# Gated-DeltaNet heads and adaLN modulation in a two-layer trunk: the 16x16 solve as its own stage, and the modulation product gathered over K

## The chip, the core and the metric

One core of a Trainium2 chip runs the whole kernel. The metric is the device time of one execution in microseconds (us). The engines are PE (TensorE, the matrix engine), DVE (VectorE), ACT (ScalarE), POOL (GpSimd) and SP (SyncE, which here only issues transfers). Each takes its own instructions strictly in order and waits for the others through semaphores.

## What is computed

A trunk of two layers, for one prompt of 1024 tokens and eight samples of 8 tokens each (1088 columns in all), with a model width of 1024. Layer 0 mixes tokens with a gated delta rule (GDN, eight heads), layer 1 with a gated linear recurrence (HGRN2, eight heads); each is followed by a convolutional feed-forward block (ConvFFN, 2816 wide). Six modulation vectors for each layer come from one product with the conditioning vectors. Cut to what matters here:

```
cs = silu(c)                                        # 9 conditioning rows (prompt + 8 samples)
for layer in range(2):
    mod = cs @ ada_w[layer] + ada_b[layer]          # 1024 x 6144: sh1, sc1, g1, sh2, sc2, g2
    h = rmsnorm(x) * (1 + sc1) + sh1
    out = gdn(h) or hgrn(h)
    x = x + (1 + g1) * rmsnorm(out)
    h = rmsnorm(x) * (1 + sc2) + sh2
    x = x + (1 + g2) * rmsnorm(conv_ffn(h))

# gated delta rule, per head and chunk of 64 tokens
A = strict_lower(kb @ k.T) * decay
sol = triangular_solve(A + I, [v * beta, kb * exp(G)])
u = uv - w @ S;  o = qg @ S + attn @ u;  S = S * gl + kd.T @ u
```

## The kernel before

**Order.** The program is written in stages, and a list scheduler sets the order on each engine from that written order and the dependences; afterwards an engine never overtakes. A GDN head is a generator, `gdn_head`, with seven stages separated by `yield`: (1) project k, convolve it; (2) decay matrices, k times k, transposes of k, and the solve; (3) project q, multiply it with k and with its decay; (4) project v and the gate g; (5) the merge; (6) the recurrence over eight 128-token tiles; (7) the samples and the output. The main loop interleaves two heads: `stage(h, 2 if h else 3)` brings head h through q and v, then come stage 1 of head h+1, stage 5 of head h, stage 2 of head h+1, and stages 6 and 7 of head h. So the solve of head h+1 is written ahead of the recurrence of head h, and the dense projection matmuls of h+1's q fill PE between the small ones of the recurrence.

**The solve.** The inverse of each 128x128 triangular block is built up from 16x16 blocks. Stage 2 writes the masked k times k to DRAM and reads the 72 diagonal blocks back as one block per partition (Zp, Ep; Ep by a POOL transfer). L794 multiplies them (`fs<-fs,Ep`; fs holds Zp, Lp and the result). L799 and L801 are 15 pairs of a small multiply and a reduce, each needing the one before; L802 copies the result; two transfers on POOL's queue write it to DRAM (`td`, L804) and read it back in the merge's layout (`mg`, L805); four ACT operations mask it (L815, L816). The merge, stage 5, begins with 32x32 matmuls `pV` (L882), whose operand those ACT operations finish, and a DVE product with EM (L875, L883).

**Modulation.** `ada_half` takes 512 of the 1024 rows of ada_w by 256 columns: four matmuls (four K blocks in the four 32-row column groups of PE), a copy by ACT, and later `ada_flush`, in which matmuls with a selector (`sel9`, L158) add the four groups up and DVE adds bias or the earlier half (L161). A 256-column piece has two halves. `ada_step` places four halves in each GDN head, with a flush for each; the ConvFFN of layer 0 takes 16 and the HGRN heads 32, there with one flush for two halves. The first two vectors of layer 0 are made in the prologue.

**Dense matmuls.** Projections and feed-forward go through `dense`: weights and activations are split into a high and a low part, three matmuls for each (L113 to L115), 384, 384 and 320 columns wide.

In time the span is: prologue to about 125 us, eight GDN heads of some 95 us to 906, output projection and norms to 1060, first ConvFFN to 1760, HGRN heads 1890 to 2430, second ConvFFN from 2580 to about 3300.

Of the kernel before, what the change touches and what calls it, by code (L numbers as in the profile page):

```python
# [14 lines left out]
ALU = mybir.AluOpType  # L15
# [27 lines left out]
def trunk_kernel(ctx: ExitStack, tc: tile.TileContext, a: dict, o: dict):  # L43
# [107 lines left out]
    def ada_flush(pt=None):  # L151

        if not ada_late:
            return
        l, c, add, sb = ada_late.pop(0)
        p2 = (pt or ps("mx", name="adap2"))[:, 256:274]
        for j in range(2):
            mm(p2[:, 9 * j:9 * j + 9], sb[:, 128 * j:128 * j + 128], sel9, start=True, stop=True)  # L158
        m = mods[l][:, 2 * c:2 * c + 2, :]
        base = m if add else adab[:, l, 2 * c:2 * c + 2].unsqueeze(2).to_broadcast([128, 2, 9])  # L160
        nc.vector.tensor_tensor(m, p2.rearrange("p (j r) -> p j r", r=9), base, op=ALU.add)  # L161


    def mod(l, i):
# [297 lines left out]
    def ffn(l, hgs, step, nxt, hname, extra, post=None):  # L462
# [3 lines left out]

        def ada_next(extra):
            if extra:
                ada_half(*extra.pop(0), "D10", "mx", True)

        def gate(f, xtag="xp", ctag=None):

# [60 lines left out]
        for c, fs in enumerate(CHUNKS[:-1]):  # L533
            if c == 0:
                gates_up(fs[:3])
                ada_next(extra)
            for f in fs[3 if c == 0 else 0:]:
                gate_up(f)
                ada_next(extra)
            for m in range(8):  # L540
                w = load_w(a["w_dn"][l, c, m], 512, "wd") if len(fs) == 4 else load_w(a["w_d3"][l, 0, m], 384, "wd")
                if c == 0:
                    acc[m] = big(f"A{m}", [128, NT], name=f"facc{m}")
                if c == 0 and m % 2:
# [152 lines left out]
        nc.vector.scalar_tensor_tensor(dst, xp, 1.0, dst, op0=ALU.add, op1=ALU.mult)  # L697
        return xp

    rest = [(0, c, hf) for c in range(8, 24) for hf in range(2)]  # L700

    def ada_step():
        ada_half(*rest.pop(0), "D10", "mm")

    def gdn_head(h):
        par = h % 2
# [84 lines left out]
            out=Zp, in_=zd[par].rearrange("t x -> (t x)").rearrange("(b y) -> b y", y=2064)[:, :2048].rearrange(  # L791
                "b (j i) -> b j i", i=128)[:, :, 0:16])
        nc.gpsimd.dma_start(out=Ep, in_=ed[par])
        nc.vector.tensor_tensor(Lp, Zp.rearrange("p j i -> p i j"), Ep.unsqueeze(2).to_broadcast([72, 16, 16]), op=ALU.mult)  # L794
        nc.gpsimd.memset(Tp, 0.0)
        nc.gpsimd.memset(fs[:72, 512 + 16:1024:33], 1.0)
        for i in range(1, 16):
            pri = fs[:72, 0:i * i].rearrange("p (c j) -> p c j", j=i)
            nc.vector.tensor_tensor(pri, Tp[:, 0:i, 0:i].rearrange("p j c -> p c j"),  # L799
                                    Lp[:, i:i + 1, 0:i].to_broadcast([72, i, i]), op=ALU.mult)  # L800
            nc.vector.tensor_reduce(Tp[:, i, 0:i], pri, axis=mybir.AxisListType.X, op=ALU.add)  # L801
        nc.vector.tensor_copy(Xp, Tp.rearrange("p i c -> p c i"))  # L802
        mg = big("D7", name="mg")
        nc.gpsimd.dma_start(out=td[par], in_=fs[:72, 512:1024])  # L804
        nc.gpsimd.dma_start(out=mg[:, 0:288].rearrange("p (t x) -> p t x", x=32),  # L805
                            in_=td[par].rearrange("(t k) (r x) -> (k r) t x", k=8, x=32))

        cp = mg[:, 0:288].rearrange("p (t i c) -> p t i c", i=2, c=16)
        XTc = mg[:, 288:800].rearrange("p (t i e c) -> p t i e c", i=2, e=2, c=16)
        Xs = mg[:64, 800:832]  # L810
        x32 = mg[:, 288:800].rearrange("p (t i c) -> p t i c", i=2, c=32)
        Xc, Tc = x32[:, :, 0, :], x32[:, :, 1, :]
        EM, V = [mg[:, i:i + 256].rearrange("p (t c) -> p t c", c=32) for i in (0, 832)]
        for e in range(2):
            nc.scalar.activation(XTc[:, :, :, e, :], cp[:, 0:8], AF.Copy, scale=m16e[:, e:e + 1])  # L815
            nc.scalar.activation(Xs[:, 16 * e:16 * e + 16], cp[:64, 8, 0, :], AF.Copy, scale=m16e[:64, e:e + 1])  # L816
        yield

        q = A(0, "q")
# [22 lines left out]
        nc.sync.dma_start(out=eg, in_=gd[1, h:h + 1, :].to_broadcast([128, NTOK]))  # L842
        nc.vector.tensor_tensor(q, q, eg, op=ALU.mult)
        qg = q

        yield

# [252 lines left out]
    ohl0 = [drp.tile([128, 2, NTOK], F32, name=f"ohl0{h}") for h in range(H)]  # L1100

    for h in range(H):
        stage(h, 2 if h else 3)
        stage(h + 1)
        stage(h)
        stage(h + 1)
        stage(h, 2)
    ada_flush()
    fold_scale(0, 2, 1)
    fold_scale(0, 4, 2)  # L1110
    fold_scale(0, 5, 3)
    hgs = out_proj(0, ohl0, 0, 2, 3, 4, "h1")
    rest = [(1, c, hf) for c in range(24) for hf in range(2)]

    def folds1():
        ada_flush()
# [27 lines left out]
    def ada_more():  # L1144
        if rest:
            ada_half(*rest.pop(0), "D10", "rc", True)

    def hgrn_head(h):
        par = h % 2
# [36 lines left out]
        if h:  # L1186
            make(1, lambda: evac_f)
            bounds()
            make(0, lambda: evac_silu(q))
            make(2, lambda: evac_v)  # L1190
            make(3, lambda: evac_silu(gt))
        else:
            ws = [load_w(a["w_hin"][h, kind], 1024, "wi", t)
                  for kind, t in ((1, ("whl", "whl")), (0, ("whl", "D1")), (3, ("D2", "D3")))]
            proj_first([(w, "pp", e) for w, e in zip(ws, (evac_f, evac_silu(q), evac_silu(gt)))], hgs)
            ada_more(), ada_more(), ada_more()
            bounds()
            v = A(2, "v")
            make(2, lambda: evac_v)
# [141 lines left out]

    for h in range(H):
        hgrn_head(h)
    ada_flush()
    fold_scale(1, 2, 1)
    fold_scale(1, 4, 2)
    fold_scale(1, 5, 3)
# [129 lines left out]
```

## Time and profile before

| | us |
|---|---|
| three runs | 3360.63, 3363.62, 3363.94 |
| median | 3363.62 |
| the profiled execution, device time | 3376.47 |
| its span in the trace | 3374.4 |
| PE busy | 3225.3 (96%) |
| DVE busy | 1658.4 (49%) |
| ACT busy | 1102.4 (33%) |
| POOL busy | 294.2 (9%) |
| granted TensorE clock, mean | 0.972 of full speed |

The profiled execution takes 2.1 us more than its span and is 12.9 us (0.38%) above the median of the three runs. "Busy" PE includes the time in which matmuls run at a lower granted clock, so a full row says only that PE had something in it. Idle time is read from the list of waits, which gives for each engine the line that waited and the operation whose end released it.

### The profile page before, as it was taken

The page shows a single profiled execution, that of the slowest core. Times are in us where ns is not written, and L with a number is a line of the kernel's source. Part 1 is how long each engine was busy: PE and PEld are TensorE (multiplying, and loading weights), DVE is VectorE, ACT ScalarE, POOL GpSimd, SP SyncE. Part 2 cuts the span into 40 slices and gives each one's busy share as a digit, 9 for nine tenths or more (in the row PEclk, how much of TensorE's full clock was granted, in tenths as well). Part 3 has the DMA queues.
Part 4 walks back from the last instruction along what each step waited for, and adds up shares of the span by engine and source line. Part 5 has one row for each costly group of instructions (what it writes and reads, how often), then busy time and mean ns, then how long its engine had stood idle before and what let it go on. Part 6 is the DMA issues. An engine that isn't in the chain of part 4 may idle for free.

```text
span 3374.4 us, 62374 instructions
## 1 busy us (share of the span) xinstructions
PE 3225.3 (96%) x25725; PEld 3007.1 (89%) x25725; DVE 1658.4 (49%) x3844; ACT 1102.4 (33%) x2521; POOL 294.2 (9%) x647
## 2 busy tenths in 40 slices
PE   7899999999989999999998999999998999999998
PEld 5788888887979999999996899898897999999997
DVE  6566566665474233333437644555456233333345
ACT  4334333433343322222234322233244332322222
POOL 0211111111020000000001000000011000000002
PEclk9989999998989999999998999999999999999999
DMA  6332223325332221111123232222532111111113
GB/s 202 90 82 86 79 86 99 96 95 166 100 104 76 85 64 45 45 45 47 43 67 116 78 103 90 88 81 85 179 120 74 44 48 45 45 45 45 43 60 105
DMA packets 195356, 278.01 MB, mean 82 GB/s; under 512 B 20056, under 2 KB 132440, under 8 KB 195072
## 3 DMA queue, kind: packets, MB, share of 16 engines
q1 hardware_dynamic: 176048, 236.24, 22.1%
q0 software_dynamic: 15616, 37.15, 3.7%
q8 instruction: 202, 3.31, 0.4%
q10 hardware_dynamic: 3408, 0.63, 0.1%
q14 instruction: 82, 0.67, 0.1%
HBM read 222.48 MB, written 51.47 MB: 81 GB/s over the span
## 4 chain that ended last, share of the span: by engine, by line
PE 85%; issue 6%; DMA 4%; DVE 3%; POOL 1%; ACT 1%; ACTq 0%; SPq 0%; POOLq 0%; DVEq 0%
PE pp L113 7%; PE pp L115 7%; PE pp L114 7%; PE pg L113 5%; PE pg L114 5%; PE pu L113 5%; PE pg L115 5%; PE pu L115 5%; PE pu L114 5%; PE pd L113 5%; PE pd L115 4%; PE pd L114 4%; PE adap L142 1%; PE pf L113 1%; PE pf L114 1%
## 5 line engine op out<-in xcount | busy, mean ns | idle before, releaser
L113 PE MATMUL pp<-h,wi 128*128 128x384 f32 (+1 forms) x1536 | 527.6, 345 | 3.9 <-ACT h L263 2.5
L115 PE MATMUL pp<-h,wi 128*128 128x384 f32 (+1 forms) x1536 | 525.9, 343 | 0.8 <-issue 0.8
L114 PE MATMUL pp<-h,wi 128*128 128x384 f32 (+1 forms) x1536 | 523.7, 341 | 1.9 <-DVE h L264 0.9
L113 PE MATMUL pg<-h,wg 128*128 128x384 f32 (+1 forms) x1056 | 346.5, 329 | 0.0
L114 PE MATMUL pg<-h,wg 128*128 128x384 f32 (+1 forms) x1056 | 346.0, 328 | 0.4 <-DVE h L264 0.4
L115 PE MATMUL pg<-h,wg 128*128 128x384 f32 (+1 forms) x1056 | 346.4, 328 | 0.0
L113 PE MATMUL pu<-h,wu 128*128 128x384 f32 (+1 forms) x1056 | 345.5, 327 | 0.0
L115 PE MATMUL pu<-h,wu 128*128 128x384 f32 (+1 forms) x1056 | 344.9, 327 | 0.0
L114 PE MATMUL pu<-h,wu 128*128 128x384 f32 (+1 forms) x1056 | 344.5, 326 | 0.0
L113 PEld LDWEIGHTS pp<-h,wi 128*128 128x128 f32 x1536 | 297.7, 194 | 23.2 <-issue 15.8
L115 PEld LDWEIGHTS pp<-h,wi 128*128 128x128 f32 x1536 | 297.6, 194 | 13.0 <-issue 10.7
L114 PEld LDWEIGHTS pp<-h,wi 128*128 128x128 f32 x1536 | 299.2, 195 | 9.8 <-issue 4.5
L113 PE MATMUL pd<-mh,wd 128*128 128x384 f32 (+1 forms) x912 | 298.5, 328 | 0.0
L115 PE MATMUL pd<-mh,wd 128*128 128x384 f32 (+1 forms) x912 | 297.6, 327 | 0.0
L114 PE MATMUL pd<-ml,wd 128*128 128x384 f32 (+1 forms) x912 | 297.3, 326 | 0.0
L113 PEld LDWEIGHTS pg<-h,wg 128*128 128x128 f32 x1056 | 199.6, 189 | 3.5 <-issue 2.9
L114 PEld LDWEIGHTS pg<-h,wg 128*128 128x128 f32 x1056 | 199.5, 189 | 1.9 <-issue 1.2
L113 PEld LDWEIGHTS pu<-h,wu 128*128 128x128 f32 x1056 | 198.2, 188 | 2.9 <-issue 2.9
L115 PEld LDWEIGHTS pg<-h,wg 128*128 128x128 f32 x1056 | 199.5, 189 | 0.0
L115 PEld LDWEIGHTS pu<-h,wu 128*128 128x128 f32 x1056 | 198.2, 188 | 0.0
L114 PEld LDWEIGHTS pu<-h,wu 128*128 128x128 f32 x1056 | 198.2, 188 | 0.0
L557 DVE TENSOR_TENSOR facc<-facc,pd 128x384 f32<-128x384 f32 (+1 forms) x192 | 97.5, 510 | 189.0 <-PE pd L115 189.0
(442 smaller groups left out, 5829.2 us busy)
## 6 DMA issues: line engine op xcount, KB each, us to landing
adaw<-in_ada_w SPq DMA_DIRECT2D x96, 512.0 KB, 4.1
wgr<-in_w_gu SPq DMA_DIRECT2D x88, 256.0 KB, 2.6
wur<-in_w_gu SPq DMA_DIRECT2D x88, 256.0 KB, 2.5
wir<-in_w_gin SPq DMA_DIRECT2D x64, 256.0 KB, 2.6
wdr<-in_w_dn SPq DMA_DIRECT2D x64, 256.0 KB, 2.6
wir<-in_w_hin SPq DMA_DIRECT2D x64, 256.0 KB, 2.9
og<-ohl SPq DMA_DIRECT2D x32, 384.0 KB, 7.2
xg<-xd SPq DMA_DIRECT2D x24, 384.0 KB, 4.8
```

The costliest lines, as they stand in the source:

```text
L113: mm(out, wh, rh(k), start=(first and i == 0), stop=False)
L114: mm(out, wh, rl(k), start=False, stop=False)
L115: mm(out, wl, rh(k), start=False, stop=(last and i == len(ks) - 1))
L142: mm(pt[32 * q:32 * q + 32, :256], cs[:, 4 * hf + q, :], w[:, q, :], start=not (keep and hf), stop=not (keep and not hf), tile_position=(0 ...
L557: nc.vector.tensor_tensor(am, am, p[:, :n], op=ALU.add)
```

## The change

The solve leaves stage 2. Everything from the multiply L794 to the four ACT operations becomes a stage of its own after the q projection, and the main loop runs `stage(h, 3 if h else 4)`. The first operation is told to keep its place in program order. The solve of head h is so written after the recurrence of head h-1 and before head h's v.

The modulation product keeps its columns and its number format, but is cut along K instead of along columns: `ada_row` takes 128 rows of ada_w by 1024 columns (a whole modulation vector), four column slices in the four column groups; eight such rows add up to the vector, in PSUM where the buffer is held, or in SBUF by a DVE addition where it is not. `ada_turn` then transposes the sum with two matmuls and adds the bias. `ada_half` stays for the two vectors of the prologue. The GDN heads now take 24 rows (three vectors of layer 0, four rows in each of the heads 0 to 5), the first ConvFFN takes 56 rows (the last vector of layer 0 and all six of layer 1; at every second m of each chunk), the HGRN heads none.

```diff
+    def ada_row(l, i, k, tag, ptag, held):
+        w = big(tag, [128, 1024], name="adaw")
+        nc.sync.dma_start(out=w, in_=a["ada_w"][l, k * 128:(k + 1) * 128, i * 1024:(i + 1) * 1024])
+        if held and k:
+            pt = ada_acc[0]
+        else:
+            pt = ps(ptag, name="adap")
+            ada_turn(None if held else pt)
+        for q in range(4):
+            mm(pt[32 * q:32 * q + 32, :256], cs[:, k, :], w[:, 256 * q:256 * q + 256], start=(not held or k == 0),
+               stop=(not held or k == 7), tile_position=(0, 32 * q))
...
+        elif not held:
+            nc.vector.tensor_tensor(ada_acc[0], ada_acc[0], pt[:, :256], op=ALU.add)
...
+    def ada_turn(pt=None):
...
+        for j in range(2):
+            nc.tensor.transpose(p2[:, 128 * j:128 * j + 128], sb[:, 128 * j:128 * j + 128], ident)
+        nc.vector.tensor_tensor(
+            mods[l][:, 8 * i:8 * i + 8, :].rearrange("p (q j) r -> p j q r", j=2),
...
-                ada_half(*extra.pop(0), "D10", "mx", True)
+                ada_row(*extra.pop(0), "D10", "rc", True)
...
-                if c == 0 and m % 2:
+                if m % 2:
                     ada_next(extra)
...
-    rest = [(0, c, hf) for c in range(8, 24) for hf in range(2)]
+    rest = [(0, i, k) for i in (2, 3, 4) for k in range(8)]
...
-        nc.vector.tensor_tensor(Lp, Zp.rearrange("p j i -> p i j"), Ep.unsqueeze(2).to_broadcast([72, 16, 16]), op=ALU.mult)
...
         nc.vector.tensor_tensor(q, q, eg, op=ALU.mult)
         qg = q
+
+        yield
+
+        tc.keep_in_program_order(nc.vector.tensor_tensor(Lp, Zp.rearrange("p j i -> p i j"), Ep.unsqueeze(2).to_broadcast([72, 16, 16]), op=ALU.mult))
...
-        stage(h, 2 if h else 3)
+        stage(h, 3 if h else 4)
...
-    ex, rest = rest[:16], rest[16:]
+    ex = [(l, i, k) for l, i in [(0, 5)] + [(1, i) for i in range(6)] for k in range(8)]
...
-            ada_more()
...
-            ada_more(), ada_more(), ada_more()
```

DVE's order at the last tiles of head 2's recurrence, where `sn` and `ru` are the steps on which PE's next matmuls wait, and where before the solve of head 3 begins (`fs`):

```order
L592 COPY ot<-po_2953 128x512
L965 SCALAR_TENSOR_TENSOR sn<-sn,eGL,pS 128x128
L644 TENSOR_TENSOR S_2505<-S_2505,eGLs 128x1024
L794 TENSOR_TENSOR fs<-fs,Ep 72x256
L950 SCALAR_TENSOR_TENSOR ru<-pKS,gc_1853,vb 128x128
L799 TENSOR_TENSOR fs<-fs 72x1
L690 SCALAR_TENSOR_TENSOR q<-gxp,c_gcw,q 128x1024
L801 TENSOR_REDUCE fs<-fs 72x1
L965 SCALAR_TENSOR_TENSOR sn<-sn,eGL,pS 128x128
```

and in the changed program:

```order
L633 COPY ot<-po_2884 128x512
L1012 SCALAR_TENSOR_TENSOR sn<-sn,eGL,pS 128x128
L685 TENSOR_TENSOR S_2477<-S_2477,eGLs 128x1024
L997 SCALAR_TENSOR_TENSOR ru<-pKS,gc_1837,vb 128x128
L731 SCALAR_TENSOR_TENSOR q<-gxp,c_gcw,q 128x1024
L184 TENSOR_TENSOR adasb<-adasb,adap 128x256
L1012 SCALAR_TENSOR_TENSOR sn<-sn,eGL,pS 128x128
L731 SCALAR_TENSOR_TENSOR q<-gxp,c_gcw,q 128x1024
```

The solve's first operation is gone from between `sn` and `ru`; an addition of the modulation row stands there instead.

DVE's order where q is scaled with its decay (`q<-q,eg`). Before, v's last convolution step and the gate follow:

```order
L839 TENSOR_SCALAR gqe<-pq 128x8
L840 TENSOR_SCALAR gqe<-pq 64x1
L843 TENSOR_TENSOR q<-q,eg 128x1088
L697 SCALAR_TENSOR_TENSOR v<-gxp,v 128x1088
L867 SCALAR_TENSOR_TENSOR g<-tg,pp 128x320
L107 TENSOR_TENSOR wi<-wir,wi 128x512
```

and in the changed program:

```order
L861 TENSOR_SCALAR gqe<-pq 64x1
L864 TENSOR_TENSOR q<-q,eg 128x1088
L869 TENSOR_TENSOR fs<-fs,Ep 72x256
L731 SCALAR_TENSOR_TENSOR v<-gxp,c_gcw,v 128x1024
L874 TENSOR_TENSOR fs<-fs 72x1
L184 TENSOR_TENSOR adasb<-adasb,adap 128x256
L876 TENSOR_REDUCE fs<-fs 72x1
L731 SCALAR_TENSOR_TENSOR v<-gxp,c_gcw,v 128x1024
```

The solve begins here, its small steps one by one between those of v and g.

DVE's order at the end of the solve in the changed program (L877 is its copy; `mg` L922 and L930 belong to the merge):

```order
L874 TENSOR_TENSOR fs<-fs 72x225
L107 TENSOR_TENSOR wi<-wir,wi 128x512
L876 TENSOR_REDUCE fs<-fs 72x15
L877 COPY fs<-fs 72x16x16
L732 SCALAR_TENSOR_TENSOR k<-gxs,c_gcw,k 128x64 x3
L184 TENSOR_TENSOR adasb<-adasb,adap 128x256
L731 SCALAR_TENSOR_TENSOR k<-gxp,c_gcw,k 128x1024
L107 TENSOR_TENSOR wi<-wir,wi 128x512
L731 SCALAR_TENSOR_TENSOR k<-gxp,c_gcw,k 128x1024
L922 TENSOR_TENSOR mg<-c_m_600,gc_2869 128x256
L731 SCALAR_TENSOR_TENSOR k<-gxp,c_gcw,k 128x1024
L930 TENSOR_TENSOR mg<-pV,mg 128x256
```

Between the solve's copy and the merge's product now lie only the convolution steps of the next head's k.

## Rows read from the trace of the kernel before

**Rows 1.** Windows (start:end, length, busy us of PE, PEld, DVE, ACT, POOL, clock, DMA share, GB/s).

```profile
352.00:447.00 95.00, 87.57 (x863) 77.60 (x862) 60.59 (x154) 37.11 (x106) 16.39 (x34) 0.96 0.30 92
1060.00:1760.00 700.00, 700.00 (x4290) 690.60 (x4289) 245.48 (x404) 184.62 (x326) 32.18 (x112) 1.00 0.18 55
1900.00:2360.00 460.00, 457.05 (x5805) 414.41 (x5803) 241.98 (x552) 145.02 (x399) 22.77 (x32) 1.00 0.27 87
```

**Rows 2.** Waits of PE, 140 to 906 us (us in total, times, longest).

```profile
PE pKS L948 <- DVE sn L965: 30.9, 5, 6.4
PE adap L142 <- DVE mod L161: 11.7, 2, 10.6
PE pus L985 <- DVE v L981: 6.0, 1, 6.0
PE pU L952 <- DVE ru L950: 6.0, 1, 6.0
```

**Rows 3.** Waits of DVE in the same stretch.

```profile
DVE fs L794 <- DMA Ep<-ed: 58.8, 8, 11.4
```

**Rows 4.** Windows (columns as in rows 1) after the gaps of heads 2 and 1.

```profile
305.50:309.30 3.80, 3.80 (x16) 3.80 (x16) 2.85 (x7) 0.27 (x1) 0.00 (x0) 0.50 0.00 0
309.30:313.10 3.80, 3.80 (x31) 3.27 (x31) 3.49 (x14) 2.80 (x4) 0.00 (x0) 0.99 0.08 16
219.60:234.20 14.60, 14.60 (x63) 11.80 (x64) 10.46 (x37) 3.40 (x10) 1.44 (x3) 0.50 0.38 119
234.20:248.80 14.60, 14.60 (x101) 14.12 (x99) 11.52 (x24) 3.79 (x5) 2.48 (x4) 1.00 0.40 127
```

**Rows 5.** Timeline of PE in an HGRN head (start, us, engine, line, operation).

```profile
2024.36 0.51 PE L158 MATMUL adap<-c_sel,adasb 128*128 128x9 f32 x4
...
2024.95 0.31 PE L114 MATMUL pp<-h,wi 128*128 128x320 f32 x1
2025.10 0.31 PE L115 MATMUL pp<-h,wi 128*128 128x320 f32 x1
2025.33 0.64 PE L142 MATMUL adap<-adaw,cs 128*32 128x256 f32 x8
...
2026.15 0.30 PE L114 MATMUL pp<-h,wi 128*128 128x320 f32 x1
```

**Rows 6.** Page, transfers: count, KB, us to landing.

```profile
adaw<-in_ada_w SPq DMA_DIRECT2D x96, 512.0 KB, 4.1
```

**Rows 7.** Timeline of PE in head 3, end of q and begin of merge.

```profile
427.95 2.05 PE L838 MATMUL pq<-ones,gxp 128*128 128x1 f32 x18
...
453.44 0.38 PE L882 MATMUL pV<-mg,Z 32*32 32x32 f32 x22
```

**Rows 8.** Timeline of DVE, heads 0, 2 and 3.

```profile
153.10 0.59 DVE L794 TENSOR_TENSOR fs<-fs,Ep 72x256 f32<-72x256 f32 x1 [11.42 <-DMA Ep<-ed]
...
163.31 0.37 DVE L802 COPY fs<-fs 72x256 f32<-72x256 f32 x1
...
324.63 0.39 DVE L802 COPY fs<-fs 72x256 f32<-72x256 f32 x1
...
401.17 0.58 DVE L794 TENSOR_TENSOR fs<-fs,Ep 72x256 f32<-72x256 f32 x1 [6.84 <-DMA Ep<-ed]
...
420.31 0.38 DVE L802 COPY fs<-fs 72x256 f32<-72x256 f32 x1
...
430.18 1.27 DVE L843 TENSOR_TENSOR q<-q,eg 128x1088 f32<-128x1088 f32 x1
```

**Rows 9.** Timeline of ACT, last mask operation of heads 2 and 3.

```profile
332.85 0.29 ACT L816 ACTIVATE mg<-mg,c_m16e 64x16 f32<-64x16 f32 x1
...
429.94 0.29 ACT L816 ACTIVATE mg<-mg,c_m16e 64x16 f32<-64x16 f32 x1
```

**Rows 10.** Timeline of POOL, the two transfers of head 3's solve.

```profile
420.99 0.56 POOL L804 DMA_DIRECT2D td<-fs  x1 [1.32 <-DVE frs L91]
...
425.82 1.03 POOL L805 DMA_DIRECT2D mg<-td  x1 [4.28 <-PE pqk L827]
```

More of the change, by code (lines that the diff above doesn't have):

```diff
@@ L161, in ada_flush @@
         nc.vector.tensor_tensor(m, p2.rearrange("p (j r) -> p j r", r=9), base, op=ALU.add)
+    ada_acc, ada_done = [], []
+    def ada_row(l, i, k, tag, ptag, held):
[9 more added lines that the diff above has]
+               stop=(not held or k == 7), tile_position=(0, 32 * q))
+        if held:
+            ada_acc[:] = [pt]
+        if k == 0 and not held:
+            ada_acc[:] = [small("adasb", [128, 256], bufs=1)]
+            nc.scalar.activation(ada_acc[0], pt[:, :256], AF.Copy)
+        elif not held:
+            nc.vector.tensor_tensor(ada_acc[0], ada_acc[0], pt[:, :256], op=ALU.add)
+        elif k == 7:
+            ada_acc[:] = [small("adasb", [128, 256], bufs=1)]
+            nc.scalar.activation(ada_acc[0], pt[:, :256], AF.Copy)
+        if k == 7:
+            ada_done.append((l, i, ada_acc.pop()))
+    def ada_turn(pt=None):
+        if not ada_done:
+            return
+        l, i, sb = ada_done.pop(0)
+        p2 = (pt or ps("mx", name="adap2"))[:, 256:512]
+        for j in range(2):
+            nc.tensor.transpose(p2[:, 128 * j:128 * j + 128], sb[:, 128 * j:128 * j + 128], ident)
+        nc.vector.tensor_tensor(
+            mods[l][:, 8 * i:8 * i + 8, :].rearrange("p (q j) r -> p j q r", j=2),
+            p2.rearrange("p (j q r) -> p j q r", q=4, r=32)[:, :, :, 0:9],
+            adab[:, l, 8 * i:8 * i + 8].rearrange("p (q j) -> p j q", j=2).unsqueeze(3).to_broadcast([128, 2, 4, 9]), op=ALU.add)
     def mod(l, i):
@@ L698, in conv_silu @@
         return xp
-    rest = [(0, c, hf) for c in range(8, 24) for hf in range(2)]
+    rest = [(0, i, k) for i in (2, 3, 4) for k in range(8)]
     def ada_step():
-        ada_half(*rest.pop(0), "D10", "mm")
+        if rest:
+            ada_row(*rest.pop(0), "D10", "mm", False)
+        else:
+            ada_turn()
     def gdn_head(h):
@@ L793, in gdn_head @@
         nc.gpsimd.dma_start(out=Ep, in_=ed[par])
-        nc.vector.tensor_tensor(Lp, Zp.rearrange("p j i -> p i j"), Ep.unsqueeze(2).to_broadcast([72, 16, 16]), op=ALU.mult)
[L795 to L816, printed above, removed]
         yield
@@ L844, in gdn_head @@
         qg = q
+        yield
+        tc.keep_in_program_order(nc.vector.tensor_tensor(Lp, Zp.rearrange("p j i -> p i j"), Ep.unsqueeze(2).to_broadcast([72, 16, 16]), op=ALU.mult))
+        nc.gpsimd.memset(Tp, 0.0)
+        nc.gpsimd.memset(fs[:72, 512 + 16:1024:33], 1.0)
+        for i in range(1, 16):
+            pri = fs[:72, 0:i * i].rearrange("p (c j) -> p c j", j=i)
+            nc.vector.tensor_tensor(pri, Tp[:, 0:i, 0:i].rearrange("p j c -> p c j"),
+                                    Lp[:, i:i + 1, 0:i].to_broadcast([72, i, i]), op=ALU.mult)
+            nc.vector.tensor_reduce(Tp[:, i, 0:i], pri, axis=mybir.AxisListType.X, op=ALU.add)
+        nc.vector.tensor_copy(Xp, Tp.rearrange("p i c -> p c i"))
+        mg = big("D7", name="mg")
+        nc.gpsimd.dma_start(out=td[par], in_=fs[:72, 512:1024])
+        nc.gpsimd.dma_start(out=mg[:, 0:288].rearrange("p (t x) -> p t x", x=32),
+                            in_=td[par].rearrange("(t k) (r x) -> (k r) t x", k=8, x=32))
+        cp = mg[:, 0:288].rearrange("p (t i c) -> p t i c", i=2, c=16)
+        XTc = mg[:, 288:800].rearrange("p (t i e c) -> p t i e c", i=2, e=2, c=16)
+        Xs = mg[:64, 800:832]
+        x32 = mg[:, 288:800].rearrange("p (t i c) -> p t i c", i=2, c=32)
+        Xc, Tc = x32[:, :, 0, :], x32[:, :, 1, :]
+        EM, V = [mg[:, i:i + 256].rearrange("p (t c) -> p t c", c=32) for i in (0, 832)]
+        for e in range(2):
+            nc.scalar.activation(XTc[:, :, :, e, :], cp[:, 0:8], AF.Copy, scale=m16e[:, e:e + 1])
+            nc.scalar.activation(Xs[:, 16 * e:16 * e + 16], cp[:64, 8, 0, :], AF.Copy, scale=m16e[:64, e:e + 1])
         yield
@@ L1107, in trunk_kernel @@
         stage(h, 2)
-    ada_flush()
     fold_scale(0, 2, 1)
     fold_scale(0, 4, 2)
-    fold_scale(0, 5, 3)
     hgs = out_proj(0, ohl0, 0, 2, 3, 4, "h1")
-    rest = [(1, c, hf) for c in range(24) for hf in range(2)]
     def folds1():
-        ada_flush()
+        ada_turn()
+        fold_scale(0, 5, 3)
         fold_scale(1, 1, 0)
-    ex, rest = rest[:16], rest[16:]
+    ex = [(l, i, k) for l, i in [(0, 5)] + [(1, i) for i in range(6)] for k in range(8)]
     hgs = ffn(0, hgs, 1, (1, 1, 0), "h2", ex, folds1)
@@ L1142, in trunk_kernel @@
     ohl1 = [drp.tile([128, 2, NTOK], F32, name=f"ohl1{h}") for h in range(H)]
-    def ada_more():
-        if rest:
-            ada_half(*rest.pop(0), "D10", "rc", True)
     def hgrn_head(h):
@@ L1343, in trunk_kernel @@
         hgrn_head(h)
-    ada_flush()
     fold_scale(1, 2, 1)
```

## The prediction

> **What bounds the kernel now.** I read the windows by stage first. In the first ConvFFN PE is busy in 700 us of 700 at full clock, in the HGRN heads in 457 of 460; a GDN head leaves 7.4 of its 95 us idle, at a mean clock of 0.96 [rows 1]. So in the feed-forward and in HGRN only PE's own work counts, and in the GDN heads two things can be won: idle time and clock. In rows 1 the reader is to see the busy share beside the clock, since a full PE at half clock looks full too.
>
> Next, PE's waits in the GDN heads. Seven of them are some 6.1 us long: the five for `sn`, one for `v`, one for `ru`, and apart from them one of 10.6 us in which a modulation matmul waits for `mod` [rows 2]. The first seven add up to 30.9 + 6.0 + 6.0 = 42.9 us. All name small DVE operations that would take well under a microsecond, so DVE stood before something else. Its own list says before what: L794, the solve's first operation, waited 58.8 us in eight places for the transfer Ep, 11.4 in the longest [rows 3]. That one is head 0 [rows 8]; the other seven average 6.8 us. The order shows the place: the solve of the next head stands between two steps of the running recurrence, and what waits for a transfer there holds up `sn`, and so PE.
>
> Last, the clock. After head 2's gap 16 matmuls ran in 3.8 us at a granted 0.50, then 31 in the next 3.8 us at 0.99 [rows 4]: half of 3.8, about 1.8 us, was lost. After head 1's gap the low stretch lasted 14.6 us, with 63 matmuls against 101 in the next 14.6 [rows 4]: 14.6 x (1 - 63/101) = 5.5 us.
>
> **The solve moves.** Removed: the seven gaps, -42.9 us, and the low clock behind them, six times 1.8 and once 5.5, -16.3. Head 0 is kept out: its L794 stands where it stood, and its wait for Ep (10.6 us of PE) stays.
>
> Moving the start is safe by the order: L794 comes behind q's scaling, for which q's whole projection has to be done, 29 us after the old place (401.2 to 430.2 in head 3 [rows 8]). Ep has long landed then. DVE's 31 small operations cost the same, 10.0 us back to back (head 0, 153.10 to 163.68 [rows 8]); in 60.6 busy of 95 us [rows 1] DVE has room. POOL's two transfers and ACT's four operations move with them; on POOL they now stand behind the copies of q's history, which are short, and the mask operations stand ahead of the next head's activations of k on ACT. Those wait for `mg`, and PE's buffers for k's projection wait for them, but only if `mg` is late, and then the merge on PE waits as well; I price this there.
>
> What is late next is the merge. It begins 453.44 - 430.00 = 23.4 us after the last q matmul on PE [rows 7], and until then the solve has to be through. In the order of the changed program, 29 more dense matmuls stand between the two (150 for 121), two modulation products for one and one turn for two flushes: 23.4 + 29 x 0.15 + 0.76 - 0.90 + 0.45 = 28.1 us (prices below). The operand is ready after q's scaling (DVE ends 1.45 us behind the q matmul [rows 7, 8]), the solve and the way to `mg`. The solve took 401.17 to 420.69, 19.5 us, among other DVE work [rows 8]. From its copy to the last mask operation it took 9.5 us in head 3 and 8.1 in head 2 [rows 8, 9]; nearly all of it is the two transfers, the second issued 4.8 us after the first [rows 10]. Sum 1.45 + 19.5 + 9.5 = 30.5, so PE waits 2 us. I take the interleaved 19.5, not the 10.0, since in the new order too other work stands between the steps. With it the heads 1 to 6 wait 2 us each. Head 7 has no next head's k to fill in: the order leaves 119 dense matmuls and no modulation, so PE is there after 23.4 - 2 x 0.15 - 0.76 - 0.90 = 21.4 us. Its solve has fewer neighbours; two thirds of the way from 10.0 to 19.5 gives 16.4 and 27.4 in all, a wait of 6. Together 6 x 2 + 6 = +18. A pause that ends in a low clock costs 1.8 as above, at seven heads +12.6. This charge is the doubtful one: the new pauses are shorter than the old.
>
> A rule of the Trainium skill bears on the way to `mg`. The trace has 9.5 us for two POOL transfers and four ACT operations [rows 8, 9]. "DMA: Bandwidth & Descriptors", section "Anatomy of one DMA", gives about 2.0 us fixed for one transfer on this path. By that (an estimate) the way would be some 6 us and no wait would be left in heads 1 to 6; the first rival would hold. Here the trace speaks against the page's figure.
>
> **The modulation.** Prices from PE's rows in an HGRN head [rows 5]: a dense matmul is 0.15 us (2024.95 to 2025.10). Between 2025.10 and 2026.15 lie two dense and one product: 1.05 - 0.30 = 0.76. Between 2024.36 and 2024.95 lie one dense and one flush: 0.59 - 0.15 = 0.45. A turn, two 128-column transposes, I set equal to a flush; no row shows one, and at nothing or at twice the price ten turns move the sum by 4.5 us either way. A row has the same four 256-column matmuls as a half, so 0.76.
>
> - GDN heads 1 to 7: 20 rows for 28 halves, -8 x 0.76 = -6.1, and three turns for 28 flushes, -25 x 0.45 = -11.3. The DVE addition of each row is hidden by DVE's 34 idle us in a head.
> - HGRN: 32 halves and 16 flushes go, -24.3 - 7.2 = -31.5, all on a full PE [rows 1].
> - First ConvFFN: 56 rows for 16 halves, +30.4, and seven turns for eight flushes, -0.4: +30.0, also on a full PE.
>
> The last two nearly cancel: -1.5. The transfers stay hidden: 40 more of 512 KB in 700 us are 29 GB/s above the 55 of that stage, and the kernel moved 127 elsewhere [rows 1, 4]. Each lands in 4.1 us [rows 6] while a row comes every 12 us. If that cover failed, PE would stand up to 4.1 us at each of 56 rows; the spare bandwidth excludes it.
>
> **Sum,** against the profiled 3376.5 us. Gains: 42.9 + 16.3 + 11.3 + 6.1 + 1.5 = 78.1; losses 18 + 12.6 = 30.6; net -47.5, or 3329.0. The profiled execution stands 0.38% above the median of the runs (3363.62 / 3376.47 = 0.9962), so the forecast is 3329.0 x 0.9962 = **3316 us**.
>
> **Rivals.**
>
> - *Nothing is late next.* The merge's operand is there before 28.1 us if solve and way take under 26.7, that is a solve below 17.2 with a way of 9.5, inside 10.0 to 19.5. For it speaks that head 3's 19.5 lay in a busy recurrence; against it that the new order threads the steps between v's convolution and the gate's operations, which wait for PE and ACT. Then -78.1: 3298.4 x 0.9962 = 3286 us.
> - *The wait moves, whole.* The solve takes 4.2 us longer than 19.5, because each small step stands behind a DVE operation that waits for PE's next group. PE then waits at the merge as long as it did before: 6 x (6.2 + 1.8) and 11.8 in head 7, +59.8, net -18.3: 3345 us. Against it: no window shows DVE that full. Beside it, the Trainium skill, "SBUF — State Buffer", section "SBUF: two separate sides", has a VectorE operation in its two-port mode lock GpSimd out of writing descriptors, 620 ns becoming 3100. That would lengthen both transfers by an estimated 2.5 us and give this case. The transfers were issued in 0.56 and 1.03 us beside a DVE that was busy two thirds of the time [rows 1, 10], so here the trace does not bear it out.
> - *PE waits for DVE during the solve.* v's last convolution step, the gate and the weights' low parts (L107) now stand between or behind 31 dependent steps. If PE finds these late, it loses the solve's own 10.0 us in each of seven heads, +70, on top of the 30.6: -78.1 + 100.6 = +22.5, or 3386 us, slower. It decides from 11.2 us per head (78.1 / 7). For it: the same queue cost 6 us a head before. Against it: then DVE waited idle for a transfer, now each step runs at once, and the order puts other work between them.
>
> That the change does not do what it says is no case: the order shows the solve gone from the recurrence and no modulation left in HGRN.
>
> **How the numbers follow.** Chances: forecast 0.58, nothing late 0.15, the wait moved whole 0.16, slower 0.11. The forecast's own range is 3299 (nothing for the clock, turns at nothing) to 3328 (turns at twice the price, 1 us more a head at the merge). For 8 in 10 the range takes in the first rival and the second, 3283 to 3347; left out are the third and the tails. A measurement of this kernel tells 0.2% (6.7 us) from no change. Faster by more: the forecast, the first rival and nearly all of the second, 0.88; within: 0.04, from the edges of the second and third; slower by more: the rest of the third, 0.08.
>
> **What would show it.** Right: no wait of PE for `sn`, `ru` or `v` of 6 us in heads 1 to 7, a list of DVE's waits in which the solve's first operation has some 11 us and not 59; HGRN heads some 31 us shorter and the first ConvFFN 30 us longer; a wait of PE at pV for the last mask operation, about 2 us, longer in the last head. Waits at pV of 6 us or none would show the second or the first rival. PE waiting for `wi`, `g` or `v` between q and the merge would show the third. The prediction is wrong altogether if the feed-forward grows by far more than 30 us, which would mean that the rows' transfers or their held buffer stop PE.

## The result

The changed kernel took 3328.26 us (median of 3336.92, 3326.15, 3330.37, 3323.36) beside 3363.78 us for the kernel before: ratio 0.9895, interval 0.987 to 0.9921, that is 35.5 us less. Run once more in a later group of runs, where the kernel before stood at 3378.35 us, it took 3331.01 us: ratio 0.9857, interval 0.9843 to 0.987. The forecast was 3316 us, a ratio of 0.9858 to the median known then. It was right in direction and kind, and 12 us too low in the first group. Between the two groups the kernel before moved by 14.6 us and the changed one by 2.8; what moved it isn't shown, so the gain is known as 35 to 47 us. One of seven executions of `longer_solve` below (5221.78 us, granted clock 0.607) is left out of its ratio.

The profiled execution took 3336.92 us, span 3335.1; profile against profile the change is 39.6 us, where the sum had 47.5.

### The profile page after: what moved, and what is told of

Its sections match the earlier page's. It is cut to its first block, busy times and chain, and to the rows that moved or that the text cites. A ratio compares the mean times of both kernels' runs of the same rounds, so it can differ in the third digit from the quotient of the medians.

```text
span 3335.1 us, 61843 instructions
## 1 busy us (share of the span) xinstructions
PE 3205.5 (96%) x25521; PEld 2983.3 (89%) x25521; DVE 1669.9 (50%) x3819; ACT 1086.1 (33%) x2475; POOL 289.6 (9%) x647
## 4 chain that ended last, share of the span: by engine, by line
PE 88%; DVE 5%; DMA 3%; issue 2%; ACT 1%; POOL 1%; ACTq 0%; SPq 0%; POOLq 0%; DVEq 0%
PE pp L113 7%; PE pp L114 7%; PE pp L115 7%; PE pg L113 5%; PE pu L113 5%; PE pg L115 5%; PE pg L114 5%; PE pu L115 5%; PE pu L114 5%; PE pd L113 5%; PE pd L115 5%; PE pd L114 5%; PE pf L113 1%; PE adap L176 1%; PE pf L115 1%
## 5 line engine op out<-in xcount | busy, mean ns | idle before, releaser
L113 PEld LDWEIGHTS pp<-h,wi 128*128 128x128 f32 x1536 | 297.5, 194 | 28.1 <-DVE adasb L184 9.2
```

What stands on the lines that cost most here:

```text
L113: mm(out, wh, rh(k), start=(first and i == 0), stop=False)
```

## The profile after

PE's waits in the GDN heads (columns as in [rows 2]):

```profile
PE pV L929 <- ACT mg L890: 22.5, 8, 5.5
PE pp L113 <- DVE adasb L184: 8.0, 1, 8.0
PE po L113 <- DMA og<-ohl: 2.8, 2, 2.5
```

The rows for `sn` and `ru` of [rows 2] are down to 0.6 and 0.9 us, the one for `v` is gone. In their place stands the merge, `pV`, which waits for the masked operand, in all eight heads. The 10.6 us of head 0 are now 8.0 us, at the DVE addition of a modulation row. DVE's own list has one wait left of the eight of [rows 3], head 0's:

```profile
DVE fs L869 <- DMA Ep<-ed: 9.0, 1, 9.0
```

Windows tell where the time went. Their ends are the same places in both programs: the GDN heads up to the first boundary's matmuls, the first ConvFFN, the HGRN heads, and the boundary behind them, up to the first matmul of the second ConvFFN (2541.4 us in the kernel before). Of the kernel before (columns as in [rows 1]):

```profile
125.00:906.00 781.00, 720.45 (x6851) 644.30 (x6851) 471.32 (x1216) 292.22 (x833) 119.64 (x246) 0.93 0.33 100
976.30:1760.50 784.20, 776.33 (x4752) 761.24 (x4749) 295.60 (x515) 220.37 (x391) 37.60 (x131) 0.99 0.18 56
1819.70:2475.20 655.50, 639.76 (x7462) 578.99 (x7463) 338.58 (x785) 214.79 (x560) 31.96 (x42) 0.98 0.33 105
2475.20:2541.40 66.20, 62.11 (x403) 52.83 (x402) 44.45 (x146) 25.97 (x57) 14.01 (x18) 1.00 0.33 106
```

and of the changed one:

```profile
125.00:864.00 739.00, 697.24 (x6673) 621.12 (x6673) 483.85 (x1205) 282.03 (x806) 116.83 (x246) 0.95 0.35 100
933.10:1744.70 811.60, 803.73 (x5056) 764.26 (x5053) 296.57 (x518) 220.24 (x390) 37.64 (x131) 0.99 0.25 80
1804.30:2431.00 626.70, 612.89 (x7142) 572.82 (x7143) 335.67 (x766) 209.49 (x544) 31.95 (x42) 0.97 0.25 83
2431.00:2501.00 70.00, 66.17 (x403) 55.16 (x402) 45.13 (x147) 25.97 (x57) 14.04 (x18) 0.93 0.33 106
```

The GDN heads lost 42.0 us: 18.8 of idle time (60.55 to 41.76) and 23.2 of PE's busy time, at a clock of 0.95 instead of 0.93. The first ConvFFN gained 27.4 us, HGRN lost 28.8. The boundary behind HGRN took 3.8 us longer with the same 403 matmuls, at a granted clock of 0.93 instead of 1.00. That is not the change: in the profiles of the experiments the same boundary takes 66.2 us in three kernels and 69 to 70 in the others, the solve alone among them, whose modulation is the old one.

The new wait step by step, in head 3. DVE, where the reader is to see the first step right behind q's scaling, other work between the small steps, and the copy at the end:

```profile
406.63 1.27 DVE L864 TENSOR_TENSOR q<-q,eg 128x1088 f32<-128x1088 f32 x1
407.83 0.58 DVE L869 TENSOR_TENSOR fs<-fs,Ep 72x256 f32<-72x256 f32 x1
408.34 1.26 DVE L731 SCALAR_TENSOR_TENSOR v<-gxp,c_gcw,v 128x1024 f32<-128x1024 f32 x1
409.53 0.14 DVE L874 TENSOR_TENSOR fs<-fs 72x1 f32<-72x1 f32 x1
...
429.02 0.40 DVE L877 COPY fs<-fs 72x256 f32<-72x256 f32 x1
```

POOL's two transfers (of head 3, and of head 7 for later), ACT's last mask operation of head 3, and PE from q's last product to the merge:

```profile
429.71 0.57 POOL L879 DMA_DIRECT2D td<-fs  x1 [0.82 <-DVE k L732]
...
433.47 1.02 POOL L880 DMA_DIRECT2D mg<-td  x1 [1.08 <-issue]
...
774.59 0.56 POOL L879 DMA_DIRECT2D td<-fs  x1 [22.22 <-DVE fs L877]
780.52 1.03 POOL L880 DMA_DIRECT2D mg<-td  x1 [5.37 <-issue]
```

```profile
438.81 0.29 ACT L891 ACTIVATE mg<-mg,c_m16e 64x16 f32<-64x16 f32 x1
```

```profile
404.40 2.05 PE L859 MATMUL pq<-ones,gxp 128*128 128x1 f32 x18
...
435.28 0.33 PE L115 MATMUL pp<-h,wi 128*128 128x384 f32 x1
438.96 0.75 PE L929 MATMUL pV<-mg,Z 32*32 32x32 f32 x64 [3.35 <-ACT mg L890]
```

The solve took 21.6 us (407.83 to 429.42), the way from there to the last mask 9.7, and PE, whose last dense matmul ended at 435.61, stood for 3.35 us. Over the heads 1 to 7 the solve took between 19.2 and 21.6 us.

## The experiments

All ratios are to the kernel before in the same group of runs; it stood at 3378.25, 3378.35 and 3377.98 us in the three groups. Every edited program is scheduled anew, so an edit can also move work that it doesn't name; where it did, the text says so.

**The two halves apart.** First the solve alone: the kernel before with the solve behind q's scaling, `ada_half` and `ada_flush` untouched.

```diff
         qg = q
 
         yield
+
+        tc.keep_in_program_order(nc.vector.tensor_tensor(Lp, Zp.rearrange("p j i -> p i j"), Ep.unsqueeze(2).to_broadcast([72, 16, 16]), op=ALU.mult))
...
+        yield
...
-        stage(h, 2 if h else 3)
+        stage(h, 3 if h else 4)
```

> Only the solve is moved; the modulation is left as it was (halves and flushes in the GDN heads, the first ConvFFN and HGRN). Theory 1, the gaps of the recurrence pay: the seven waits of 6.1 us for sn, ru and v go, a wait at the merge of 2 to 4 us a head comes; against the kernel before -20 to -30 us (ratio 0.991 to 0.994), that is about two thirds of the whole change. Theory 2, the modulation pays: the wait moves whole to the merge, 0 to -6 us (0.998 to 1.000).

Measured: 3335.59 us, ratio 0.987 (0.9852 to 0.9887), -43.9 us by the ratio. PE's waits:

```profile
PE pV L885 <- ACT mg L846: 9.8, 6, 6.1
```

The gaps of the recurrence are gone, and the wait at the merge is less than half of that in the whole change; the 6.1 us are head 7's, and in the heads 2 to 6 it is 1 us or less. That is more than either theory gave, and nearly as much as the whole change. In head 3 the solve, the last mask and the merge stand so:

```profile
400.93 0.58 DVE L825 TENSOR_TENSOR fs<-fs,Ep 72x256 f32<-72x256 f32 x1
...
419.70 0.39 DVE L833 COPY fs<-fs 72x256 f32<-72x256 f32 x1
```

```profile
428.31 0.29 ACT L847 ACTIVATE mg<-mg,c_m16e 64x16 f32<-64x16 f32 x1
```

```profile
428.46 0.33 PE L885 MATMUL pV<-mg,Z 32*32 32x32 f32 x16 [0.93 <-ACT mg L846]
```

PE comes to the merge no later here than in the whole change (28.0 us after the q matmul, 29.2 there). It waits less because its operand is there sooner: the solve takes 19.2 us instead of 21.6, the way to the last mask 8.5 instead of 9.7. Over the heads 1 to 7 PE's time from q to the merge is 198.6 us, and 198.8 in the whole change; the solves add up to 137.2 and 144.5 us, the ways to 62.7 and 66.9.

Then the modulation alone: the changed kernel with the solve put back into stage 2.

```diff
         nc.gpsimd.dma_start(out=Ep, in_=ed[par])
+        nc.vector.tensor_tensor(Lp, Zp.rearrange("p j i -> p i j"), Ep.unsqueeze(2).to_broadcast([72, 16, 16]), op=ALU.mult)
...
-        stage(h, 3 if h else 4)
+        stage(h, 2 if h else 3)
```

> Only the modulation is changed; the solve stays at its old place. Theory 1: the seven gaps of some 6 us stay at sn, ru and v, and the time falls by what PE is spared in the GDN heads, -10 to -17 us against the kernel before (0.995 to 0.997); the HGRN heads lose about 25 us of matmuls and the first ConvFFN gains about as much. Theory 2: -25 to -35 us (0.990 to 0.993).

Measured: 3364.87 us, ratio 0.9953 (0.9938 to 0.9969), -15.9 us by the ratio and -13.4 by the medians, within theory 1. PE's waits:

```profile
PE pKS L994 <- DVE sn L1011: 34.9, 5, 8.3
PE pus L1031 <- DVE v L1027: 8.7, 1, 8.7
PE pU L998 <- DVE ru L996: 8.4, 1, 8.4
```

The seven gaps of [rows 2] stay, and grow to 34.9 + 8.7 + 8.4 = 52.0 us from 42.9. Apart the halves give 0.0130 and 0.0047, together 0.0143 by the later measurement of the whole change (0.0105 by the first). So the modulation, worth 0.0047 alone, adds some 0.001 at most once the solve has moved, which is less than the intervals can tell from nothing.

**Does PE really wait for the solve?**

```diff
-        nc.vector.tensor_copy(Xp, Tp.rearrange("p i c -> p c i"))
+        for _ in range(9):
+            nc.vector.tensor_copy(Xp, Tp.rearrange("p i c -> p c i"))
```

> The changed kernel with the last copy of the solve made nine times instead of once: eight more copies of 0.39 us, 3.1 us more in each solve. If PE at the merge waits for the end of the solve in every head, each wait at pV grows by 3.1 us and the kernel by 8 x 3.1 = 25 us against the changed kernel (0.997 against the kernel before). If the solve has slack and the wait has another cause (the transfers' queue, the masks' place on ACT), the growth is under 8 us (0.990 to 0.992).

Measured: 3369.15 us, ratio 0.997 (0.9956 to 0.9984). Beside the changed kernel in the neighbouring group (0.9857) that is 38 us, more than the 25 put in; beside the first measurement (0.9895) it is 25.

```profile
PE pV L930 <- ACT mg L891: 34.9, 7, 17.1
PE po L113 <- DMA og<-ohl: 10.6, 2, 8.6
```

This does not settle the question, though the time fits the first branch. The waits did not grow by 3.1 us in each head: in the heads 1 to 3 they are 8.0 us together (10.3 in the changed kernel), in 4 to 6 they are 9.8 (5.5), and in head 7 17.1 (5.5). The scheduler had moved PE's work as well. Between the last q matmul and the merge the heads 1 to 6 now have 164 to 194 dense matmuls (139 to 152 before the edit), which hide part of the longer solve, and head 7 has 42 instead of 118, so that PE is there after 11.5 us instead of 29.2. Head 7's projections and some out-projection matmuls now stand ahead of q's end, the latter so early that they wait 8.6 us for their transfer. What stays is that PE found the operand late in the heads 1 to 7. Whether the merge waits for this chain is better read from the edits below, which make the operand come earlier.

**The changed kernel once more,** unedited, as a base.

> The changed kernel once more, beside the three others of this call on the same chip, as their base. Expected: 0.987 to 0.992 against the kernel before, waits at pV of 20 to 25 us in all.

Measured: 3331.01 us, ratio 0.9857; waits at pV 23.4 us.

**Where must the solve begin?** Three other places. First, a few microseconds earlier: the solve written ahead of q's projection.

```diff
+        tc.keep_in_program_order(nc.vector.tensor_tensor(Lp, Zp.rearrange("p j i -> p i j"), Ep.unsqueeze(2).to_broadcast([72, 16, 16]), op=ALU.mult))
...
         sq = project(0, q)
...
-        stage(h, 3 if h else 4)
+        stage(h, 2 if h else 3)
```

> The changed kernel with the solve written ahead of q's projection instead of behind q's scaling; in the order of DVE its first step then stands ahead of q's products with k, some 4 to 6 us earlier. If the wait at the merge is the solve's lateness, the 22.5 us of waits at pV shrink to under 8, and the kernel gains 10 to 18 us against the changed kernel (0.984 to 0.987 against the kernel before). If DVE is what is full there (the solve ends when DVE has got through v's and g's steps, wherever it begins), the waits stay within 2 us a head of what they are and the time stays (0.988 to 0.991); if the earlier steps hold up q's products, PE waits for dec or q and the kernel is slower (over 0.992).

Measured: 3333.5 us, ratio 0.987 (0.9853 to 0.9886), as the changed kernel (0.9857 and 0.9895). PE's waits and DVE's busy time (third after the length) in head 3's solve:

```profile
PE pV L927 <- ACT mg L862: 22.1, 8, 4.6
```

```profile
402.06:425.16 23.10, 23.10 (x154) 22.38 (x153) 20.45 (x55) 7.32 (x19) 1.82 (x4) 1.00 0.37 133
```

The solve began 2.2 us ahead of the end of the q matmul instead of 1.4 behind it, and took 23.1 us instead of 21.6, with DVE busy in 20.5 of them: the steps that it overtook now stand between its own. Of the 3.6 us some 2 arrived at its end in head 3, 0.6 in head 2 and 0.7 in the mean of the heads 1 to 7. The waits at pV moved by 0.8 us a head and less, in the heads 0 and 1 by +1.4 and -2.1. That is the second branch of the expectation for the waits: the solve ends where DVE has got through the steps around it. The ratio stands at the edge of the first branch's range; the changed kernel was not run in this group.

Second, directly behind the recurrence of the head before, some 15 us earlier, as a stage between recurrence and samples:

```diff
-        stage(h, 3 if h else 4)
+        stage(h, 2 if h else 4)
         stage(h + 1)
         stage(h)
         stage(h + 1)
-        stage(h, 2)
+        stage(h)
+        stage(h + 1)
+        stage(h)
```

> The changed kernel with the solve written directly behind the recurrence of the head before (between that recurrence and its samples) instead of behind q's scaling; its first step stands on DVE three or four rows behind the last sn, some 15 us earlier than in the changed kernel. Theory, the operand of the merge is late and DVE is full between q's scaling and the merge: between the recurrence and q's scaling DVE has room, the solve is through before v's steps begin, the waits at pV fall from 22 to under 4 us and the kernel gains 15 to 25 us against the changed kernel (0.982 to 0.986 against the kernel before). Rival: Ep has not landed there, DVE stands for it, and the samples and the finish behind it hold PE: waits for DVE of 3 us or more a head come back and the gain is under 8 us (0.987 or more).

Measured: 3319.29 us, ratio 0.9822 (0.9808 to 0.9835), 11.7 us below the changed kernel of the same group: the ratio lies in the first range, the gain is less than the 15 us forecast and more than the rival's. DVE in head 3, and PE's waits:

```profile
395.58 0.57 DVE L840 TENSOR_TENSOR fs<-fs,Ep 72x256 f32<-72x256 f32 x1
```

```profile
PE pp L113 <- DVE adasb L184: 14.3, 3, 8.6
PE pv L766 <- DVE v L738: 5.6, 7, 1.0
PE pV L930 <- ACT mg L861: 3.1, 2, 2.2
```

The wait at pV is nearly gone, and Ep had landed here, except in head 1, where DVE stood for it for 7.3 us once more (the rise of `adasb` from 8.7 to 14.3). It is the earlier start that helps, not room on DVE: the solve of head 3 takes 21.2 us here too, with DVE busy in 20.4 of them, but it ends 7.0 us behind the last q matmul instead of 23.0. What was not gained are that gap and the 0.8 us a head for v's convolution.

Third, without the mark; the scheduler then puts the first operation back into the recurrence.

```diff
-        tc.keep_in_program_order(nc.vector.tensor_tensor(Lp, Zp.rearrange("p j i -> p i j"), Ep.unsqueeze(2).to_broadcast([72, 16, 16]), op=ALU.mult))
+        nc.vector.tensor_tensor(Lp, Zp.rearrange("p j i -> p i j"), Ep.unsqueeze(2).to_broadcast([72, 16, 16]), op=ALU.mult)
```

> The changed kernel without the mark that keeps the solve's first operation in program order: in DVE's order that operation then stands again two to nine rows ahead of the last sn of the running recurrence. If standing in the recurrence is what costs (DVE waits there for Ep), gaps of 2 to 8 us at sn, ru or v come back in each head and the kernel loses 10 to 25 us against the changed kernel (0.992 to 0.997). If the place does no harm since Ep has landed by then, the waits at pV fall and the kernel gains (under 0.988).

Measured: 3357.01 us, ratio 0.9926 (0.9914 to 0.9939), 26 us slower than the changed kernel.

```profile
PE pKS L995 <- DVE sn L1012: 24.2, 6, 5.3
PE pus L1032 <- DVE v L1028: 9.5, 1, 9.5
```

```profile
DVE fs L869 <- DMA Ep<-ed: 46.5, 8, 10.1
```

Moving the stage in the text is not enough. Half of the gain (0.0069 of 0.0143) hangs on the mark that holds the one operation which waits for a transfer.

**The way to the operand.** Both transfers of the solve by SP instead of POOL:

```diff
-        nc.gpsimd.dma_start(out=td[par], in_=fs[:72, 512:1024])
-        nc.gpsimd.dma_start(out=mg[:, 0:288].rearrange("p (t x) -> p t x", x=32),
+        nc.sync.dma_start(out=td[par], in_=fs[:72, 512:1024])
+        nc.sync.dma_start(out=mg[:, 0:288].rearrange("p (t x) -> p t x", x=32),
```

> The changed kernel with the two transfers between the solve and the masks issued by SP instead of POOL. If POOL's issue is what makes the way from the solve's copy to the masks 8.7 us long, the way falls by 2 us or more, the waits at pV fall from 22 to under 10 us, and the kernel gains 8 to 15 us against the changed kernel (0.984 to 0.988). If the transfers themselves are what takes the time, the way stays within 1 us, and the time within 5 us. If SP, which waits for the solve's copy in its turn, holds up the weight loads behind it, PE waits for wi and the kernel is slower than the changed one.

Measured: 3317.1 us, ratio 0.9813 (0.9799 to 0.9826), 13.9 us below the changed kernel; again in the next group, as its base:

> The changed kernel with the solve's two transfers issued by SP, once more, as the base of this call. Expected 0.980 to 0.985 against the kernel before, waits at pV of some 5 us in all.

3315.24 us, 0.9813 (0.979 to 0.9836). PE's waits, then SP's issues and ACT's last mask operation of head 3:

```profile
PE pV L929 <- ACT mg L890: 5.3, 7, 1.4
```

```profile
415.73 0.32 SPq L879 DMA_DIRECT2D td<-fs  x1
418.91 0.39 SPq L880 DMA_DIRECT2D mg<-td  x1
```

```profile
422.42 0.29 ACT L891 ACTIVATE mg<-mg,c_m16e 64x16 f32<-64x16 f32 x1
```

From the first issue to the last mask 7.0 us, by POOL 9.4 (429.71 to 439.10). Over the heads 1 to 7 the ways add up to 48.3 us instead of 66.9, and the waits at pV fell by 18 us. No wait of PE for weights has come up behind SP's queue. In head 7 a wait of 4.0 us at pX has come in its place; the profile names nothing that ended it. Here too the order moved: in head 1 the merge has 113 dense matmuls ahead of it instead of 139.

Now the question whether the modulation was given back at that wait: the solve alone as above, with the two lines of its transfers edited as here.

> The solve moved and its two transfers issued by SP, with the modulation as it was in the kernel before. With POOL's transfers the new modulation was worth little once the solve had moved (the kernel with the solve alone stood within 0.2% of the whole change). If that is because PE, spared in the GDN heads, only waited longer at pV, then with that wait gone the modulation is worth again what it was alone: this kernel is 9 to 16 us slower than the base of this call (0.985 to 0.988 against the kernel before). If the modulation gives nothing beside the moved solve for another reason (dearer rows, DVE's additions), this kernel stands within 5 us of the base.

Measured: 3333.85 us, ratio 0.9867 (0.9851 to 0.9883), 18.6 us slower than the base, a little more than the 9 to 16 expected. PE's wait for the masked operand is all but gone:

```profile
PE pX L894 <- issue: 7.1, 4, 3.3
PE pV L885 <- ACT mg L846: 0.2, 1, 0.2
```

So beside a merge that hardly waits the modulation is worth 0.0054, as much as alone. The GDN heads with the solve alone, by POOL's transfers and by SP's (columns as in [rows 1]; the whole change is above):

```profile
125.00:861.10 736.10, 702.48 (x6846) 624.63 (x6846) 483.34 (x1211) 290.86 (x833) 116.14 (x246) 0.97 0.37 106
```

```profile
125.00:861.40 736.40, 708.77 (x6832) 629.86 (x6832) 482.51 (x1208) 291.52 (x833) 102.46 (x230) 0.96 0.37 106
```

With POOL's transfers the whole change has 41.8 us of idle time there and the solve alone 33.6, with 12.7 us more at pV, and its granted clock is 0.95 instead of 0.97, so that PE's busy time is only 5.2 us shorter. Idle time and clock together take back what PE has less to do. What lengthened the wait is the later operand shown above, not an earlier PE. Why the chain is longer beside the new modulation is not shown.

One thing does not fit a simple count of waits. With the old modulation the two lines took 9.6 us of waiting at pV away, and the time stayed (0.987 and 0.9867): idle time fell by 6.0 us and PE's busy time rose by 6.3, at a clock of 0.96 instead of 0.97. The two intervals leave some 8 us either way, so a gain as large as the wait is not excluded, but it is not shown; the 13.9 us above hold for the changed kernel.

Both remedies together:

> Both remedies together: the solve directly behind the recurrence and its transfers issued by SP. If both take away the same wait at pV, the two together give no more than the better one: within 6 us of the base of this call. If each takes away something of its own, the kernel gains 10 us or more against the base.

Measured: 3316.97 us, ratio 0.9818 (0.9802 to 0.9835), as the base. Neither adds to the other; that both take away the same wait fits this. And the transfers ahead of the solve by SP too:

```diff
-        nc.gpsimd.dma_start(out=ed[par].rearrange("(t k) i -> (k i) t", k=8), in_=nE)
+        nc.sync.dma_start(out=ed[par].rearrange("(t k) i -> (k i) t", k=8), in_=nE)
...
-        nc.gpsimd.dma_start(out=Ep, in_=ed[par])
+        nc.sync.dma_start(out=Ep, in_=ed[par])
```

> The base of this call with the transfers ed and Ep, ahead of the solve, issued by SP too. In head 0 DVE waits some 9 us for Ep and PE after it, in the first modulation row, for 8 us; ed takes 10 us from its issue to the issue of Ep. If the issue by POOL makes ed slow, the wait of head 0 falls by 2 us or more and the kernel gains 2 to 6 us. If ed's many small pieces make it slow, nothing changes in head 0; SP's queue then only stands longer, and the kernel is the same or slower by up to 10 us.

Measured: 3316.11 us, ratio 0.981 (0.979 to 0.9829), as the base. In head 0 DVE's wait for Ep fell:

```profile
DVE fs L869 <- DMA Ep<-ed: 7.7, 1, 7.7
```

from 10.5 us in the base, and PE's behind it from 8.4 to 5.6; 2.8 us are below what the runs can tell in the time. SP's issues in head 0:

```profile
136.64 0.38 SPq L825 DMA_DIRECT2D ed<-gc  x1
147.52 0.38 SPq L837 DMA_DIRECT2D Ep<-ed  x1
```

`ed` holds back Ep's issue for 10.9 us here, and for 10.5 by POOL in the base, so POOL's issue is not what makes it slow. It is Ep that got quicker: DVE began 1.5 us after its issue (at 149.07) instead of 4.5.

## Why the prediction was right, and which terms were off

**The gaps.** Right: all seven are gone, for the reason given; with the solve put back they are back. That head 0 keeps its wait was right too; it moved to `adasb` and lost 2.6 us.

**The order as argument.** Right, and stronger than I put it: with the mark left out the same stage order gives half the effect.

**The wait at the merge.** Right in kind, 22.5 us for 18, of which 1.3 in head 0 had no place in the sum. In head 3, counted from the end of the q matmul (406.45): PE there after 29.2 us for 28.1, the solve begun after 1.4 for 1.45, 21.6 us long for 19.5, the way 9.7 for 9.5, a wait of 3.35 for 2. The solve was mis-sized. I took its length from one head, and that was the shortest of the heads 1 to 7 of the kernel before (19.5 us; the others took 20.1 to 24.6). (The 10.0 us back to back were 10.6 in the rows, which hardly counts.) It is not that DVE was less loaded in that place: it was busy in 17.4 of the 19.5 us, and in 18.1 of the 21.6 in the new place. In head 7 two errors cancelled, which is luck. PE took 782.67 - 753.5 = 29.2 us to the merge for 21.4. The matmuls were those that I had counted (118 in the trace, 119 in the order; 69 of them are the out-projection's), but PE stood for 3.6 us among them, 2.5 of these for the out-projection's transfer, and the granted clock was low:

```profile
753.45:782.67 29.22, 25.63 (x128) 23.30 (x128) 16.93 (x47) 5.43 (x10) 1.92 (x3) 0.88 0.78 267
```

The operand came later too: the solve took 19.5 for 16.4, and the second transfer stood 5.9 us behind the first instead of 4.8, so that the way was 14.0 for 9.5. Forecast 6, measured 5.5.

**The clock.** The doubtful charge of 12.6 us behind the new waits was too high, not empty. The granted clock was 0.50, the lower of its two levels, after PE had waited at pV in the heads 1, 2, 3 and 7, for 15.7 us in all, so that some 7.8 us were lost; in the heads 4 to 6 it stayed at 1.00. The heads' mean clock rose from 0.93 to 0.95, some 18 us less lost (0.07 x 781 against 0.05 x 739, to the rounding of two digits), where the sum had 16.3 - 12.6 = 3.7. A part of this is chance: two profiles of the kernel with SP's transfers differ by 7 us of PE's busy time in these heads (690.55 and 697.95), at 0.96 and 0.95. PE's busy time there fell by 23.2 us, where modulation and clock together had 17.4 + 16.3 - 12.6 = 21.1. The boundary of 66 us that fell from 1.00 to 0.93 gave 3.8 back; no step had it, and it does so in kernels with and without the change.

**The sum.** For the GDN heads it had 46.0 us and the profile shows 42.0: busy time 2.1 better, idle time 18.8 less instead of 24.9 less, by the merge (4.5 more than forecast) and the out-projection's transfer (2.8), against 2.6 won in head 0. The boundary's 3.8 make up the other half of the 8 us between 47.5 and 39.6.

**The modulation.** First ConvFFN +27.4 for +30.0, HGRN -28.8 for -31.5: both prices a tenth too high, the difference -1.4 for -1.5. With the -6.1 and -11.3 of the GDN heads the modulation had 18.9 us in the sum; alone it gave 15.9, while the seven gaps took 9.1 more. Adding it to the solve's terms was the step that failed: on top of the moved solve it gave 0.0013, some 4 us. The sum's terms for the solve, 42.9 + 16.3 - 18 - 12.6 = 28.6 us, were as far off the other way, for the solve alone gave 43.9: beside the old modulation the waits at the merge were 9.8 us and not 18. So the total was nearer than its two parts, and that is luck.

**The rivals.** The first (nothing late next) needed a solve below 17.2 us; none in the heads 1 to 7 was (19.2 the shortest). Its time, 3286, was not reached by any kernel. Putting the transfers on SP comes near to what it describes, mostly by a shorter way (48.3 us over the heads 1 to 7 for 66.9; the solves 137.7 for 144.5): wait at pV 5 us, ratio 0.9813. The Trainium skill, "DMA: Bandwidth & Descriptors", section "Specifications", gives a first-byte latency of about 1 us for POOL's path and 0.6 for SP's, 0.8 us for two transfers (an estimate); the trace has 2.4 us in head 3 (9.4 against 7.0). The direction agrees, the size is three times as large. The second rival asked for a solve 4.2 us longer; the longest was 2.1 longer. The third did not come: the rows by which PE waits for `v` or `g` between q and the merge are 0.6 us and less.

## What to carry to other kernels

An operation that waits for a transfer does its harm through what stands behind it in its engine's order; when it is moved, look for what waits for the end of its chain, and take the chain's length from several heads and not from one: here it was 10.6 us back to back and 17.3 to 21.6 with other work between its 31 steps, at one and the same place in the text. Two changes that each pay alone need not add up while an operand is late: here the second gave 0.001 beside the wait at the merge and 0.005 without it, so remove the wait first and then measure. In a scheduled program the written place is only a wish; read the order, and read it again after each edit, PE's too, for a few more copies on DVE took 76 of 118 dense matmuls out of the stretch in which PE covers the last solve.

## What the runs showed of the hardware

- A pair of dependent transfers through DRAM with four mask operations took 9.4 us issued by POOL and 7.0 issued by SP, in the same head of two kernels whose source differs in these two lines; through all heads PE's wait for them was 22.5 and 23.4 us by POOL, 5.3 and 5.1 by SP.
- `ed`, 1152 single values of 4 bytes scattered to DRAM, kept its successor from issuing for 10 us, as POOL's rows of head 0 in the changed kernel show:

```profile
136.32 1.04 POOL L825 DMA_DIRECT2D ed<-gc  x1
...
146.30 0.57 POOL L837 DMA_DIRECT2D Ep<-ed  x1 [8.94 <-DMA ed<-gc]
```

  Issued by SP it did so for 10.9 us in head 0 (the rows above). Over all heads it was 10.0 to 12.5 us by POOL in the changed kernel and 9.0 to 10.9 by SP.

- The granted clock of one boundary was 1.00 or 0.93 to 0.95, with the same 403 matmuls in it and with no relation to the edit (66.2 us in the kernel before and three others, 69 to 70 in the rest). Differences of 3 us in a stage of 66 us may be nothing but that.
